# Attention in a two-block hybrid layer stack: products on the whole TensorE array, and the causal mask as a POOL select

## The chip, the cores and the metric

The kernel runs on one core of a Trainium2 chip as one launch. The metric is the time on the device in microseconds, taken as the median of the runs. The core has five engines with queues of their own: TensorE for products, VectorE, ScalarE and GpSimd (POOL) for the rest, and SyncE, which issues the DMAs.

## What is computed

256 tokens of 1024 channels go through a first block (a gated delta rule, a linear recurrent unit and an MLP), get 16 meta tokens put before them, and go through two layers of a second block. Each of these layers is a SwiGLU, a mixer and another SwiGLU. The change touches the mixer, and in it the attention with 8 heads of 64 channels:

```python
proj = u @ w_in
q, k, v, a, b, g_sb, g_conv = jnp.split(proj, IN_SPLITS, axis=-1)
y_sb = stick_breaking_attention(q, k, v) @ w_attn_out
y_conv = conformer_conv(a, b, conv_w, conv_b, conv_ln_g, conv_ln_b) @ w_conv_out
m = jax.nn.sigmoid(g_sb) * y_sb + jax.nn.sigmoid(g_conv) * y_conv
return m @ w_out
# stick_breaking_attention, z = q k^T / sqrt(64), valid = key < query:
log_keep = jnp.where(valid, jax.nn.log_sigmoid(-z), 0.0)
after = lax.cumsum(log_keep, axis=3, reverse=True) - log_keep
attn = jnp.where(valid, jnp.exp(jax.nn.log_sigmoid(z) + after), 0.0)
out = attn @ v
```

So each weight is sigmoid(z) times the product of sigmoid(-z) over the keys between key and query, and keys at or behind the query count as 1 in the product and as 0 in the result.

## The kernel before

**The weight stream.** All weight matrices come from memory in one fixed order, in chunks of 2048 columns, and are cut into units of up to eight 128x128 tiles. ScalarE rounds a unit to its high part (`wh`, float32r), VectorE or, for some units (`POOLED`, line 32), POOL takes the difference (`wl`, line 284 and line 491). TensorE makes three products for each tile, high by high, high by low and low by high (lines 532 to 534, in `job`), over the 272 or 256 tokens. This stream is nearly all of TensorE's work.

**The order of issue.** Every engine works its queue in order, and the order is laid out when the program is built, by a planner in the kernel: each helper (`act`, `tt`, `mm`, `tr` and others) adds an expected cost to its engine's clock by `op` (line 249). Side work is written as generators (`start_flow`, line 332), which `tick` (line 384) advances after each tile of the stream when the operands are expected to be ready. Splits of weights are laid out up to three units ahead of TensorE (`emit_split`, line 481). The conv steps of the mixer are fillers: they are laid wherever VectorE's clock isn't ahead of TensorE's.

**The mixer (from line 1458).** Channels are on the partitions, tokens on the columns. Jobs of the stream come in this order: a and b, q and k, v, the gates gc and gs (8 tiles each), then `ys` (attention output), `yc` (conv output) and `o2`. The side work is the conv over 31 taps on VectorE (`conv`, line 1520), its layer norm, the values, and the heads. Scratch comes from one tile, `arena` (line 146), and nine slots of temporaries, `tmp` (line 378).

- `keep` (line 1494) copies a finished query tile from PSUM to `QT`; a tile of 128 channels holds two heads, one on partitions 0 to 63 and one on 64 to 127.
- `values` (line 1568) transposes the values and scales them into `VN`.
- `head` (line 1582) does one head: for each block of query tokens (16, 128 and 128 in layer 0, 128 and 128 in layer 1) the scores against all keys up to the block's end, over 16, 144 and 272 columns, with 64 rows of the array; then a bfloat16 product of the identity with a mask of -1e30, added to the scores; two sigmoids on ScalarE, a scan and a multiplication on VectorE, transposes on TensorE, three copies on ScalarE, and three products with the values, each with a stationary operand of 64 columns, into the head's half of the partitions of a bank that both heads of a pair share.
- `heads` (line 1658) runs the heads of one parity one after the other; the two parities are two flows.

## Time and profile before

| | us |
|---|---|
| median of 3 timed runs | 1558.58 |
| lowest and highest of them | 1553.17, 1559.71 |
| span of the profiled execution | 1560.1 |
| TensorE busy in it | 1528.2 |
| VectorE busy | 1065.3 |
| ScalarE busy | 800.1 |
| POOL busy | 164.4 |

For the profiled execution the page gives the span, from the first to the last instruction, and no time of its own beside it; the runs of the median are other executions of the same program. TensorE's busy time counts an instruction from its start to its modelled end, and neighbours overlap, so the pace of the products is read from the distance between starts. The granted clock stands as a share of the full 2.4 GHz, of which 1.2 GHz is the other level; its mean over the span is 0.988.

### The profile page before, as it was taken

The numbers are of one execution on the slowest core, as the hardware profiler recorded it, in microseconds if no ns is written. First come the engines' busy times: TensorE is split into PE (matmuls) and PEld (weight loads), VectorE is DVE, ScalarE is ACT, GpSimd is POOL, SyncE is SP. The second block draws the span as 40 slices with busy tenths as digits, with TensorE's granted clock in tenths as the row PEclk, the third lists the DMA queues.
The fourth block names the chain that finished last, engine by engine and source line by source line (L and its number), as shares of the span: only waits on it lengthen the run. The fifth ranks groups of instructions, "written<-read, shape, count | busy, mean of one in ns | idle before, by whom it ended". The sixth has DMA issues, their size and how long they took to land.

```text
span 1560.1 us, 29338 instructions
## 1 busy us (share of the span) xinstructions
PE 1528.2 (98%) x12160; PEld 1488.3 (95%) x12160; DVE 1065.3 (68%) x1884; ACT 800.1 (51%) x1351; POOL 164.4 (11%) x146
## 2 busy tenths in 40 slices
PE   7999999999999999999999999999999999999997
PEld 7898999999999999889999999999999989999997
DVE  5887866667555578877765555655558976866654
ACT  4568666544444444545544444444444555555443
POOL 3230300000000011114400000000001113500000
PEclk8999999999999999999999999999999999999999
DMA  6312555554545543323555454554554423555552
GB/s 227 136 55 82 184 187 183 183 184 164 188 163 176 176 162 135 136 86 131 175 178 188 155 174 157 191 187 160 172 183 160 162 84 109 175 204 190 183 174 76
DMA packets 36373, 248.75 MB, mean 159 GB/s; under 512 B 3984, under 2 KB 5264, under 8 KB 12304
## 3 DMA queue, kind: packets, MB, share of 16 engines
q1 hardware_dynamic: 35248, 245.63, 44.5%
q8 instruction: 95, 1.56, 0.4%
q10 hardware_dynamic: 992, 1.26, 0.2%
q14 instruction: 38, 0.31, 0.1%
HBM read 245.82 MB, written 1.05 MB: 158 GB/s over the span
## 4 chain that ended last, share of the span: by engine, by line
PE 90%; DVE 6%; ACT 2%; issue 1%; POOL 0%; DMA 0%; POOLq 0%; DVEq 0%; SPq 0%; ACTq 0%
PE bank L532 28%; PE bank L534 27%; PE bank L533 27%; PE bank L315 6%; DVE arena L295 2%; DVE arena L284 1%; PE bank L319 1%; DVE wl L284 1%; ACT arena L272 1%; DVE H L284 1%; ACT wh L272 1%; DVE x L284 0%; DMA H<-in_xt_dram 0%; POOL acc L307 0%; DVE co L284 0%
## 5 line engine op out<-in xcount | busy, mean ns | idle before, releaser
L532 PE MATMUL bank<-x,wh 128*128 128x272 f32 (+1 forms) x2624 | 766.9, 292 | 11.5 <-ACT x L272 10.6
L534 PE MATMUL bank<-x,wl 128*128 128x272 f32 (+1 forms) x2624 | 756.0, 288 | 3.6 <-DVE wl L284 3.4
L533 PE MATMUL bank<-x,wh 128*128 128x272 f32 (+1 forms) x2624 | 754.7, 288 | 2.3 <-DVE x L284 1.6
L284 DVE TENSOR_TENSOR wl<-raw,wh 128x1024 fp32r<-128x1024 f32 (+4 forms) x453 | 528.5, 1168 | 207.0 <-PE bank L534 168.8
L272 ACT ACTIVATE wh<-raw 128x1024 fp32r<-128x1024 f32 (+4 forms) x510 | 495.6, 977 | 279.6 <-PE bank L533 219.7
L532 PEld LDWEIGHTS bank<-x,wh 128*128 128x128 f32 x2624 | 500.5, 191 | 16.1 <-ACT x L272 11.7
L533 PEld LDWEIGHTS bank<-x,wh 128*128 128x128 f32 x2624 | 503.4, 192 | 5.0 <-DVE x L284 2.9
L534 PEld LDWEIGHTS bank<-x,wl 128*128 128x128 f32 x2624 | 500.1, 191 | 4.7 <-DVE wl L284 4.7
L534 PE MATMUL bank<-hid,wl 128*128 128x272 f32 (+1 forms) x960 | 273.8, 285 | 0.0
L532 PE MATMUL bank<-hid,wh 128*128 128x272 f32 (+1 forms) x960 | 273.6, 285 | 0.0
L533 PE MATMUL bank<-hid,wh 128*128 128x272 f32 (+1 forms) x960 | 273.0, 284 | 0.0
L532 PEld LDWEIGHTS bank<-hid,wh 128*128 128x128 f32 x960 | 180.9, 188 | 0.0
L533 PEld LDWEIGHTS bank<-hid,wh 128*128 128x128 f32 x960 | 180.9, 188 | 0.0
L534 PEld LDWEIGHTS bank<-hid,wl 128*128 128x128 f32 x960 | 180.5, 188 | 0.0
L491 POOL TENSOR_TENSOR wl<-raw,wh 128x512 fp32r<-128x512 f32 (+3 forms) x57 | 106.6, 1884 | 321.4 <-ACT wh L272 171.4
L284 DVE TENSOR_TENSOR tmp<-bank,R 128x272 f32<-128x272 f32 (+1 forms) x184 | 78.8, 430 | 69.2 <-PE bank L534 66.9
L272 ACT ACTIVATE tmp<-tmp 128x272 f32<-128x272 f32 (+1 forms) x140 | 59.3, 425 | 115.4 <-DVE tmp L284 78.5
L295 DVE SCALAR_TENSOR_TENSOR bank<-arena,C,bank 128x272 f32<-128x272 f32 (+1 forms) x232 | 102.0, 492 | 4.9 <-ACT bank L272 3.8
L1482 POOL MEMSET arena<- 128x1 f32 x10 | 0.5, 99 | 779.1 <-PE bank L534 779.1
L315 PE MATMUL bank<-arena 128*128 128x128 f32 (+7 forms) x528 | 77.6, 286 | 1.1 <-ACT arena L272 0.9
L284 DVE TENSOR_TENSOR hid<-tmp,hid 128x272 fp32r<-128x272 f32 (+1 forms) x120 | 51.7, 433 | 38.1 <-ACT hid L272 38.1
L272 ACT ACTIVATE x<-H,C 128x272 fp32r<-128x272 f32 (+2 forms) x64 | 30.0, 486 | 87.7 <-DVE H L284 87.2
(210 smaller groups left out, 1068.4 us busy)
## 6 DMA issues: line engine op xcount, KB each, us to landing
raw<-in_w_dram SPq DMA_DIRECT2D x187, 1024.0 KB, 4.8
raw<-in_w_dram SPq DMA_DIRECT2D x32, 960.0 KB, 4.7
raw<-in_w_dram SPq DMA_DIRECT2D x16, 896.0 KB, 4.6
raw<-in_w_dram SPq DMA_DIRECT2D x2, 512.0 KB, 5.9
H<-in_xt_dram SPq DMA_DIRECT2D x1, 544.0 KB, 6.6
LG<-in_lgw_dram SPq DMA_DIRECT2D x1, 512.0 KB, 6.3
out_dram<-H SPq DMA_DIRECT2D x2, 256.0 KB, 2.2
LM<-in_cm_dram SPq DMA_DIRECT2D x1, 448.0 KB, 5.5
```

Source lines behind the costliest of these rows:

```text
L272: nc.scalar.activation(out, in_, func, scale=scale, **kw)
L284: nc.vector.tensor_tensor(out=out, in0=a, in1=b, op=fn)
L295: nc.vector.scalar_tensor_tensor(out=out, in0=a, scalar=s, in1=b, op0=op0, op1=op1)
L315: nc.tensor.matmul(out, lhsT, rhs, start=start, stop=stop)
L319: nc.tensor.transpose(out, in_, identity)
L491: nc.gpsimd.tensor_tensor(out=lo[:, 0:n], in0=raw[c][:, o:o + n], in1=wh[i][:, 0:n].bitcast(F32), op=SUB)
L532: nc.tensor.matmul(acc, h[:, s], xh, start=first and done == 0, stop=False)
L533: nc.tensor.matmul(acc, h[:, s], xl, start=False, stop=False)
L534: nc.tensor.matmul(acc, lo[:, s], xh, start=False, stop=last and done == total - 1)
L1482: nc.gpsimd.memset(a.f[:, w:w + 1], 1.0)
```

## The change

The queries are copied into two tiles `QZ`, each with one head of a pair and zeros on the other 64 partitions, so that a score product uses all 128 rows and always 128 columns of the array. The values of a head stand in `VZ` between columns of zeros, so that a product with a 128-column slice writes all 128 partitions of the pair's bank, and the six products of both heads add up in it. The first key block's weights go to `AM`, whose 112 other partitions are zeros. These tiles are filled with zeros by POOL at the start of each mixer. The mask product is gone; instead POOL sets the upper triangle of the two score maps after the sigmoids, to 1 in the one and to 0 in the other. One of the copies goes to a temporary slot instead of the arena. Comments and docstrings that were dropped are left out here.

```diff
-MIX2 = 14560
+MIX2 = 16200
...
-    identb = const.tile([128, 128], BF16, name="identb")
-    maskb = const.tile([128, 128], BF16, name="maskb")
...
-        QT, KT, VT = arena.get(4, T2), arena.get(4, T2), arena.get(4, T2)
+        KT, VT = arena.get(4, T2), arena.get(4, T2)
+        QZ = [arena.get(4, n) for _ in range(2)]
...
-        VN = arena.get(3, 512)
-        if not ready_b[0]:
-            vcopy(identb, ident)
-            vcopy(maskb, M[:, 2])
-            ready_b[0] = True
+        VZ = arena.get(3, 4, 192)
+        AM = [arena.get(n) for _ in range(2)]
+        for i in range(2):
+            nc.gpsimd.memset(QZ[i].f[64 * (1 - i):64 * (1 - i) + 64], 0.0)
+            nc.gpsimd.memset(AM[i].f, 0.0)
+        nc.gpsimd.memset(VZ.f, 0.0)
...
+        def keep_q(t, b, ev):
+            for i in range(2):
+                p = slice(64 * i, 64 * i + 64)
+                cp(QZ[i].f[p, t], b[p, 0:n])
+            give(b)
+            note(ev)
+            yield "V"
...
-                act(VN.f[0:sn, i], b[0:sn], AF.Copy, scale=RC[0:sn, i:i + 1])
+                for par in range(2):
+                    p = slice(64 * par, 64 * par + 64)
+                    act(VZ.f[0:sn, i, :, 128 * par:128 * par + 64], v4(b[0:sn])[:, :, p], AF.Copy, scale=RC[0:sn, i:i + 1])
...
+        def before(a, fill):
+            nc.gpsimd.affine_select(
+                out=a, in_=a, pattern=[[-1, a.shape[-1]]], compare_op=ALU.is_gt, fill=fill, base=0,
+                channel_multiplier=1,
+            )
+            op("G", 0.15 + 0.001 * a.shape[-1])
...
-                z = b[0:tn, col:col + S]
-                mm(z, QT.f[p0:p0 + 64, hp, t0 - o:t0 - o + tn], KT.f[p0:p0 + 64, hp, 0:S], stop=False)
-                mm(z[:, t0:S], identb[0:tn, 0:tn], maskb[0:tn, 0:tn], start=False)
+                mm(b[:, col:col + S], QZ[par].f[:, hp, t0 - o:t0 - o + 128], KT.f[:, hp, 0:S])
...
                 act(a.f[0:tn, 0:S], z, AF.Sigmoid, scale=RP[0:tn, bi:bi + 1])
+                before(keeps[i][0:tn, t0:S], 1.0)
+                before(a.f[0:tn, t0:S], 0.0)
...
-            at_b = arena.get(656)
-            at = at_b.f
+            at_b = arena.get(128)
+            at = yield from slot()
...
-            cp(at[0:NM, 384:384 + n], b1[0:NM, 0:n])
-            cp(at[:, 256:384], b1[:, 288:416])
+            cp(AM[par].f[0:NM], b1[0:NM, 0:n])
+            cp(at_b.f, b1[:, 288:416])
...
-            vs = slice(128 * hp + p0, 128 * hp + p0 + 64)
+            V = VZ.f[:, :, hp, 64 * par:64 * par + 128]
             e = n - 256
-            mm(py[p0:p0 + 64, 0:n], VN.f[0:NM, 0, vs], at[0:NM, 384:384 + n], stop=False)
-            mm(py[p0:p0 + 64, e:n], VN.f[:, 1, vs], at[:, 0:256], start=False, stop=False)
-            mm(py[p0:p0 + 64, e + 128:n], VN.f[:, 2, vs], at[:, 256:384], start=False)
+            mm(py[:, 0:n], V[:, 0], AM[par].f, pairs[hp][1] == 0, False)
+            mm(py[:, e:n], V[:, 1], at[:, 0:256], False, False)
+            mm(py[:, e + 128:n], V[:, 2], at_b.f, False, pairs[hp][1] == 1)
             at_b.done()
+            free_tmps.append(at)
...
-            start_flow(keep(QT.f[:, t, 0:n], job("q", x, n, o), ev_q[t]))
+            start_flow(keep_q(t, job("q", x, n, o), ev_q[t]))
```

## Rows read from the trace of the kernel before

**Rows 1.** This is the first part of the page: busy time of each engine, its share of the span, and the count of its instructions (PE is TensorE, PEld its weight loads, DVE VectorE, ACT ScalarE, POOL GpSimd).

```profile
PE 1528.2 (98%) x12160; PEld 1488.3 (95%) x12160; DVE 1065.3 (68%) x1884; ACT 800.1 (51%) x1351; POOL 164.4 (11%) x146
```

**Rows 2.** This is the fourth part of the page: the shares of the engines in the chain of work that ended last.

```profile
PE 90%; DVE 6%; ACT 2%; issue 1%; POOL 0%; DMA 0%; POOLq 0%; DVEq 0%; SPq 0%; ACTq 0%
```

**Rows 3.** This is the windows view of four stretches: start and end in us, length, then busy time and instruction count of PE, PEld, DVE, ACT and POOL, the granted clock, the DMA share and GB/s. The first and third are the stretches of the heads in layer 0 and layer 1, the second and fourth what follows them up to the end of the gates.

```profile
598.00:692.00 94.00, 94.00 (x654) 79.62 (x653) 76.31 (x166) 49.34 (x119) 11.96 (x5) 0.98 0.32 113
692.00:716.00 24.00, 24.00 (x186) 23.51 (x185) 14.16 (x39) 9.84 (x20) 5.25 (x3) 1.00 0.27 91
1204.00:1294.00 90.00, 90.00 (x639) 77.66 (x638) 76.55 (x158) 48.73 (x104) 11.92 (x5) 0.98 0.35 124
1294.00:1316.00 22.00, 21.88 (x179) 21.47 (x179) 15.09 (x36) 10.59 (x24) 4.98 (x3) 1.00 0.29 104
```

**Rows 4.** This is the timeline of TensorE in layer 0 around the score products of one head: start in us, duration of one or end of the last less start of the first where several are merged, engine, line, operation, operands, tile shape, count. L315 is the helper of the kernel's own products, L532 to L534 the weight stream. A product in float32 (not float32r) is two instructions.

```profile
647.20 0.29 PE L532 MATMUL bank<-x,wh 128*128 128x272 f32 x1
...
647.45 0.29 PE L534 MATMUL bank<-x,wl 128*128 128x272 f32 x1
647.67 0.21 PE L315 MATMUL bank<-arena 64*16 64x16 f32 x2
...
648.51 0.72 PE L315 MATMUL bank<-arena 64*128 64x272 f32 x2
...
649.21 0.37 PE L532 MATMUL bank<-x,wh 128*128 128x272 f32 x1
649.41 0.29 PE L533 MATMUL bank<-x,wh 128*128 128x272 f32 x1
```

**Rows 5.** This is the timeline of TensorE at three places where float32 products use all 128 rows: the layer norm's means, a sum over the channels, and the transposes of a head in layer 1 (two of these five have 16 columns).

```profile
700.33 2.00 PE L315 MATMUL bank<-arena,mean 128*128 128x272 f32 x8
...
702.29 0.28 PE L533 MATMUL bank<-x,wh 128*128 128x272 f32 x1
...
568.12 0.72 PE L315 MATMUL bank<-ones,acc 128*128 128x1 f32 x6
...
568.92 0.29 PE L533 MATMUL bank<-x,wh 128*128 128x272 f32 x1
...
1253.53 0.71 PE L319 MATMUL bank<-M,arena 128*16 128x128 f32 x5
...
1254.20 0.28 PE L533 MATMUL bank<-x,wh 128*128 128x256 f32 x1
```

**Rows 6.** This is the same view in layer 1: the stream products before and behind one head's score products (from 1246.22 to 1247.93) and one head's value products (from 1256.08 to 1257.88).

```profile
1246.22 0.28 PE L534 MATMUL bank<-x,wl 128*128 128x256 f32 x1
...
1247.93 0.28 PE L533 MATMUL bank<-x,wh 128*128 128x256 f32 x1
...
1255.84 0.28 PE L532 MATMUL bank<-x,wh 128*128 128x256 f32 x1
...
1256.08 0.28 PE L534 MATMUL bank<-x,wl 128*128 128x256 f32 x1
...
1257.88 0.28 PE L533 MATMUL bank<-x,wh 128*128 128x256 f32 x1
```

**Rows 7.** This is the same view in layer 0: the stream products before and behind the value products of one head (666.08 and 667.92) and of two heads in a row (638.98 and 642.22).

```profile
666.08 0.29 PE L534 MATMUL bank<-x,wl 128*128 128x272 f32 x1
...
667.92 0.29 PE L533 MATMUL bank<-x,wh 128*128 128x272 f32 x1
...
638.98 0.29 PE L534 MATMUL bank<-x,wl 128*128 128x272 f32 x1
...
642.22 0.29 PE L533 MATMUL bank<-x,wh 128*128 128x272 f32 x1
```

**Rows 8.** This is the same view at the first two heads of layer 0, those of the first pair: the first product of each, and the first stream product behind them.

```profile
598.96 0.21 PE L315 MATMUL bank<-arena 64*16 64x16 f32 x2
...
600.62 0.21 PE L315 MATMUL bank<-arena 64*16 64x16 f32 x2
...
602.15 0.52 PE L532 MATMUL bank<-x,wh 128*128 128x272 f32 x1
```

**Rows 9.** This is the windows view in slices of 2 us, columns as above; the granted clock is the number behind the busy times.

```profile
602.00:604.00 2.00, 2.00 (x10) 1.89 (x10) 1.78 (x6) 2.00 (x9) 0.00 (x0) 0.56 0.76 320
604.00:606.00 2.00, 2.00 (x12) 2.00 (x11) 1.79 (x5) 2.00 (x4) 0.00 (x0) 0.59 0.00 0
1271.00:1273.00 2.00, 2.00 (x11) 1.91 (x11) 1.76 (x5) 2.00 (x6) 0.00 (x0) 0.56 1.00 393
```

**Rows 10.** This is the view of one source line, the only select on POOL: duration in ns (least, median, greatest), first and last start, shape.

```profile
L926 POOL TENSOR_SCALAR_AFFINE_SELECT arena<-arena x2: 637/728/819, 45.2 to 45.8; 128x512 f32<-128x512 f32 x2
```

**Rows 11.** This is the timeline of POOL at the start of the first mixer.

```profile
562.45 0.27 POOL L1482 MEMSET arena<- 128x1 f32 x6 [380.61 <-PE bank L534]
562.65 0.21 POOL L1483 MEMSET arena<- 128x128 f32 x1
562.82 2.39 POOL L491 TENSOR_TENSOR wl<-raw,wh 128x1024 fp32r<-128x1024 f32 x1
```

**Rows 12.** This is the timeline of VectorE at the same place; in brackets the idle time before and what ended it.

```profile
562.43 0.44 DVE L284 TENSOR_TENSOR tmp<-bank,R 128x272 f32<-128x272 f32 x1 [1.07 <-PE bank L534]
562.91 2.60 DVE L284 TENSOR_TENSOR H<-H,tmp 128x272 f32<-128x272 f32 x1
```

**Rows 13.** This is the chain that ended last, in order of time, at the same place: start, length, engine and what it writes.

```profile
562.91 2.60 DVE H L284
```

More of the change, by code (lines that the diff above doesn't have):

```diff
@@ L1454, in swiglu @@
         return nx, ev_sq, phase
-    ready_b = [False]
     def mixer(x, ev_r, layer, next_g, old_phase):
@@ L1580, in mixer @@
         pairs = {}
+        def before(a, fill):
[4 more added lines that the diff above has]
+            op("G", 0.15 + 0.001 * a.shape[-1])
         def head(hp, par):
-            p0 = 64 * par
             yield from wait(ev_q[hp], ev_k[hp])
```

## The prediction, made before the changed kernel was run

> **What bounds the kernel now.** I read the busy times first: TensorE is busy for 1528.2 of 1560.1 us, VectorE for 1065.3, ScalarE for 800.1 [rows 1]. The chain that ended last is 90% TensorE and 6% VectorE [rows 2]. So TensorE's queue sets the time, and the change has to be priced by what it does to that queue. Busy time doesn't give this price, since a TensorE counted busy may be changing over between products; the distances between starts do, so I read the timeline next.
>
> The eight heads of a layer lie between the products of the weight stream in 598 to 692 and 1204 to 1294 us. TensorE is busy in all of both; VectorE, next, for 76.3 of 94.0 and 76.6 of 90.0 us [rows 3]. That is the second thing to see: VectorE has 17.7 and 13.4 us of air there, and a TensorE that becomes 11 us faster uses up most of it.
>
> **The products.** One head of layer 0 alone: the stream product before it starts at 647.45, the second one after it at 649.41 [rows 4]. In these 1.96 us lie the head's nine instructions and two stream products. Stream products by themselves start 0.125 us apart (647.20 to 647.45 are two), so the head takes 1.96 - 2x0.125 = 1.71 us. The reader should see where it goes: the last pair of 64-row products over 272 columns with its mask product takes 649.21 - 648.51 = 0.70 us, and the first stream product behind them 0.20 instead of 0.125.
>
> With full operands the same arithmetic stands elsewhere in the trace. Eight 128x128 products over 272 columns and one stream product run from 700.33 to 702.29: (1.96 - 0.125)/8 = 0.229 us each. Six over one column take (0.80 - 0.125)/6 = 0.112 each, five over 128 columns (0.67 - 0.12)/5 = 0.110 each, the changeover behind them counted in [rows 5]. I scale 144 columns to 0.121 and 256 to 0.215. A float32 product is two instructions, so a head's scores cost 2x(0.112 + 0.121 + 0.229) = 0.92 us; the 16-column block's stationary operand grows from 16 to 128 columns and is counted at 0.112. The saving is 1.71 - 0.92 = 0.79 us a head, 6.3 us in layer 0. Layer 1 has two blocks: 1247.93 - 1246.22 - 2x0.12 = 1.47 us [rows 6] against 0.70, 0.77 a head, 6.2 us.
>
> The value products of one head alone in layer 0: 667.92 - 666.08 - 0.25 = 1.59 us; of two heads in a row: 642.22 - 638.98 - 0.25 = 2.99 [rows 7]. Padded they take 2x(0.229 + 0.215 + 0.110) = 1.11. The saving is 0.48 alone and 0.385 in a row; eight heads give 3.1 to 3.8 by how they lie, I take 3.3. In layer 1: 1257.88 - 1256.08 - 0.24 = 1.56 [rows 6] against 2x(0.215 + 0.215 + 0.110) = 1.08, 0.48 alone, 3.4 with a like mix. Transposes keep their form.
>
> Sum on TensorE: 6.3 + 3.3 + 6.2 + 3.4 = **19.2 us**, all in a queue that never idles there.
>
> A rule speaks against padding: the Trainium skill, TensorEngine Tiling (Array Packing), section Theoretical Speedup, says that products with a small side can run as independent tiles, up to twice as fast. By it the two heads of a pair would share the array, a pair of score products would take one head's time instead of the padded 1.85, a pair of value products 1.39 instead of 2.22, and padding would lose some 9 us. The row decides: the second head of a pair starts at 600.62, when the first, begun at 598.96, is through, and the next stream product at 602.15 [rows 8]. They ran in turn, 1.6 us each, so there is no overlap to lose.
>
> **The clock.** Behind these two heads the granted clock falls to 0.56 in 602 to 604 and 0.59 in 604 to 606, that is 1.2 GHz for most of it; the same begins at 1271 [rows 9]. It costs 2x0.44 + 2x0.41 = 1.7 us of full-speed work each time, 3.4 together. TensorE was busy without a pause before [rows 3]; what it did was partial-array products one after the other. I take it that full-array products keep 2.4 GHz and **3.4 us** come back; the lower bound is nothing.
>
> On this the Trainium skill, TensorE: Matmul & The Clock Gate, Part 1, says that the rate follows how busy the engine has been. By that rule a TensorE busy throughout would not have fallen, the cause would lie elsewhere, and the sum would lack the 3.4. The row shows a fall without a pause, so busy time alone doesn't explain it.
>
> **POOL and VectorE.** Each block's two score maps get a select on POOL: 48 in layer 0 (16 of them 16x16), 32 in layer 1. The nearest row is a 128x512 select, 0.73 us [rows 10]. With a fixed part of about 0.10 (six one-column fills overlap in 0.27 us [rows 11]) 128 columns come to 0.26; bounds are 0.21, the 128-column fill [rows 11], and 0.73, if width doesn't count. I take 0.26: 32x0.26 + 16x0.12 = 10.2 us of POOL in layer 0, 8.3 in layer 1, where it now works 12 us of 94 and of 90 [rows 3]. A select stands between ScalarE's sigmoid and VectorE's scan, and on POOL it is in order with weight splits of 2.39 us [rows 11]: it waits for a split ahead of it, and a split behind it waits for the sigmoid. Splits are laid out up to three units ahead of TensorE's (some 9 us), which covers a late split; conv steps cover a late scan. Without that cover it is 2.4 us a hit.
>
> POOL also stops VectorE: H<-H,tmp, with both operands in SBUF, takes 2.60 us, where the step before it over as many columns took 0.44; it starts at 562.91, inside POOL's split of 562.82, and ends with it [rows 11, 12]. Selects will do this too, shorter. About half of VectorE's time is such operations; I charge a third of the select time, 3 us a layer (from 0 to all of it). VectorE then has 79.3 and 79.6 us against a TensorE of 94.0 - 9.6 - 1.7 = 82.7 and 90.0 - 9.6 - 1.7 = 78.7. In layer 0 it fits, in layer 1 it misses by 1. Its conv work may slip into 692 to 716 and 1294 to 1316, where it works 14.2 and 15.1 us [rows 3], but two queues of fixed order that are nearly full wait for each other. I charge TensorE waits of 1 us in layer 0 and 3 in layer 1, **4 us** given back; the bounds are 0 and the whole saving.
>
> **The start of each mixer.** Fills of QZ, AM and VZ (1088, 1088, 272, 272 and 2304 columns) come to stand on POOL ahead of the split at 562.82. By the 128-column fill of 0.21 us they take 4.8 us with the fixed part, up to 8.2 without. No row shows fills beside such VectorE steps; they read nothing, so I take it that they don't stop it. Then H<-H,tmp, which is on the chain that ended last [rows 13], loses its 2.16 us of waiting. But the split, now later, will stop two-operand steps of the norm behind it, on which TensorE waits as well: I keep 0.6 a layer, **1.2 us** (up to 4.3 if the split meets nothing, -4 if fills do stop VectorE).
>
> **At nothing:** two ScalarE copies for each query tile and each block of values instead of one, 7 more a layer at the stretch's mean of 0.41 us, hidden by a ScalarE that works 49 of 94 us [rows 3] (2.9 us without that cover); two VectorE casts dropped; a temporary slot in place of a wide arena block; AM reused by the next head of its parity, whose copy waits for products long issued. DMA issues and SP's queue don't change.
>
> **Sum:** -19.2 - 3.4 - 1.2 + 4 = -19.8 us on 1560.1. The three timed runs have a median of 1558.6 and reach from 1553.2 to 1559.7; the profiled execution, of which only the span is given, lies 1.5 above the median. Off the median it is 1538.8; I round to **1540 us**.
>
> **Rivals.**
> VectorE becomes the bound: it keeps half of its air, 8.9 and 6.7 us, so the stretches end at 88 and 86 us instead of 94 and 90. Gain 5.8 + 3.7 + 1.2, 1548. For it: 81% and 85% busy now. Against it: it has other stages to slip into. Chance 0.18.
>
> The clock still falls: 3.4 less, 1543; inside the forecast, a quarter of it.
>
> Given back: the next stage stops TensorE by as much, since the conv norm arrives no earlier than now, 1555 to 1559. Against it: some 20 us of other products lie between the last head and the first product that reads the heads' results [rows 3]. Chance 0.10. That padding doesn't give the full form can hardly be, since the operands are whole.
>
> Slower: a 128-column select costs what the 512-column one does, 0.73 us. Then POOL has 35 and 23 us of selects, and VectorE, stopped for half to all of that, needs 94 to 111 and 88 to 100 us in stretches of 94 and 90: midway 13 us more than now, less 3.4 and 1.2, 1567. It decides from about 0.45 us a select. Against it: fills grow with width [rows 11]. Chance 0.07. The tiling rule's 1568 has 0.02.
>
> **Numbers.** The forecast (gain of 12 to 26) has 0.63. Faster by over 0.5%, 7.8 us and about what a measurement of this kernel can tell from no change: 0.63 and two thirds of 0.18, 0.75. Within 0.5%: 0.16. Slower: 0.09. The range goes from 1532, with all bounds in my favour, past the VectorE case to 1552; it leaves out the last rivals and a part of the tail below.
>
> **What would show it.** Scores of a head at 0.92 us with no mask product, and a stream product 0.125 behind; value products at 1.11; a granted clock of 1.00 at the heads; selects near 0.26; H<-H,tmp at 0.44. Wrong if selects take over 0.45, or if TensorE idles for VectorE's scans or splits by more than 10 us.

## The result, and the profile after

The changed kernel takes 1544.0 us (median of 6 runs, 1538.9 to 1550.1) beside 1555.9 us for the kernel before in the same set: a ratio of 0.9916, 95% interval 0.9888 to 0.9943. Two later sets of 6 runs gave 0.9894 (0.9866 to 0.9922) and 0.9915 (0.9895 to 0.9936). So it is about 0.9% faster, some 14 us; 1540 had been forecast with a range of 1532 to 1552. The profiled execution took 1550.1 us, the slowest of its six; its span is 1548.4 us, against 1560.1 us before.

The first part of the page after, to be read beside [rows 1]:

```profile
PE 1507.0 (97%) x12120; PEld 1486.7 (96%) x12120; DVE 1076.3 (70%) x1882; ACT 804.1 (52%) x1365; POOL 197.6 (13%) x236
```

TensorE is busy for 21.2 us less, but the span is only 11.7 us shorter: 9.5 us came back as pauses. Some 4 us of the 21.2 are not the change's: they belong to a pace of the last gate and up products that differs between executions of one program (last section). Where the pauses lie is seen in the windows view of the changed kernel, with the columns of [rows 3]:

```profile
598.00:692.00 94.00, 93.24 (x710) 89.70 (x710) 84.57 (x169) 53.82 (x126) 29.80 (x54) 1.00 0.38 134
692.00:716.00 24.00, 23.99 (x181) 22.95 (x181) 19.58 (x48) 8.77 (x21) 6.58 (x6) 1.00 0.26 89
1204.00:1294.00 90.00, 87.82 (x690) 84.83 (x688) 83.97 (x161) 52.05 (x114) 25.37 (x34) 1.00 0.39 136
1294.00:1316.00 22.00, 21.32 (x178) 21.12 (x178) 14.49 (x38) 13.38 (x25) 11.54 (x9) 1.00 0.32 109
```

In the heads' stretches TensorE issues more instructions in the same time (710 and 690 instead of 654 and 639), the granted clock stays at 1.00, and VectorE has gone from 76.3 and 76.6 to 84.6 and 84.0 us. TensorE, which never paused there before, now does.

**A single head.** TensorE's timeline after, around the scores of a head in layer 0, the values of one, and the scores of one in layer 1, answering to [rows 4, 6, 7]:

```profile
649.92 0.29 PE L532 MATMUL bank<-x,wl 128*128 128x272 f32 x1
650.04 1.09 PE L315 MATMUL bank<-arena 128*128 128x16 f32 x6
650.77 0.49 PE L530 MATMUL bank<-x,wh 128*128 128x272 f32 x1
651.10 0.29 PE L531 MATMUL bank<-x,wh 128*128 128x272 f32 x1
...
672.88 0.29 PE L532 MATMUL bank<-x,wl 128*128 128x272 f32 x1
...
674.25 0.29 PE L531 MATMUL bank<-x,wh 128*128 128x272 f32 x1
...
1244.23 0.28 PE L532 MATMUL bank<-x,wl 128*128 128x256 f32 x1
1244.35 0.86 PE L315 MATMUL bank<-arena 128*128 128x144 f32 x4
1244.85 0.48 PE L530 MATMUL bank<-x,wh 128*128 128x256 f32 x1
1245.17 0.28 PE L531 MATMUL bank<-x,wh 128*128 128x256 f32 x1
```

Read as the prediction read them, from the stream product before to the second one behind, less two of the stream's distances: scores 651.10 - 649.92 - 0.25 = 0.93 us (0.92 forecast), values 674.25 - 672.88 - 0.25 = 1.12 (1.11 forecast), scores in layer 1 1245.17 - 1244.23 - 0.24 = 0.70 (0.70 forecast). One sub-claim failed: the first stream product behind the scores starts its successor 0.33 us later (650.77 to 651.10), not 0.125. The changeover is dearer than before, when it was 0.20 us [rows 4]. The sum came out all the same, since the forecast had worked out its price of 0.92 us from rows with the changeover counted in [rows 5].

**Stretch by stretch.** The stream's 11,136 products come in the same order in every kernel, so their starts serve as a ruler. Four stretches hold all of the change: the 528 products up to the 32nd of each mixer ("ahead"), and the 1,248 from there on ("mixer"; a mixer has 1,248). The boundary lies about 4 us into the mixer, so that TensorE's wait for the last part of the mixer's input, which comes before the mixer's 22nd product, falls into "ahead"; the 528 products up to the mixer's first take 66.3 us in every kernel. This table is worked out from the starts of those products in each profile; pauses are TensorE's, over 0.2 us.

| profile | ahead 1 | mixer 1 | ahead 2 | mixer 2 | sum | pauses in mixer 1 / 2 |
|---|---|---|---|---|---|---|
| before | 68.0 | 201.7 | 68.0 | 191.2 | 528.9 | 1.6 / 1.9 |
| changed, first profile | 66.3 | 197.2 | 66.3 | 188.4 | 518.2 | 4.4 / 9.1 |
| changed, `again` | 66.3 | 195.7 | 66.3 | 188.5 | 516.7 | 4.4 / 9.2 |
| changed, `again_2` | 66.3 | 195.7 | 66.3 | 188.3 | 516.6 | 4.4 / 9.2 |
| `no_select` | 66.3 | 194.6 | 66.3 | 186.4 | 513.6 | 3.2 / 8.4 |
| `mask_product` | 66.3 | 195.9 | 66.3 | 189.5 | 518.0 | 5.1 / 8.0 |
| `half_select` | 68.0 | 199.7 | 68.0 | 186.6 | 522.3 | 3.0 / 3.1 |
| `o2_on_vector` | 66.3 | 195.7 | 66.3 | 183.4 | 511.6 | 4.4 / 7.0 |
| `b_on_vector` | 66.3 | 193.8 | 66.3 | 185.9 | 512.3 | 2.6 / 8.0 |
| `both_on_vector` | 66.3 | 193.2 | 66.3 | 182.1 | 508.0 | 3.2 / 4.3 |
| `both_2` | 66.3 | 193.8 | 66.3 | 182.9 | 509.4 | 2.6 / 4.2 |
| `late_fills` | 68.0 | 194.2 | 68.0 | 187.8 | 518.0 | 2.9 / 8.0 |
| `both_half_taps` | 66.3 | 189.4 | 66.3 | 181.3 | 503.4 | 1.4 / 3.5 |
| `none_in_heads` | 66.3 | 197.4 | 66.3 | 187.8 | 517.9 | 5.8 / 7.7 |

The rest of the span differs between executions of one kernel by several us, for reasons shown at the end; that is why the sums of these stretches tell more than single spans.

**Where the pauses are.** Three kinds of them make most of the difference, and behind each stands the same thing: a weight split on POOL that reads two tiles, and a VectorE step that meets it and ends with it, or up to 0.3 us behind it.

At the start of the mixer (POOL's timeline, then VectorE's, then the waits of TensorE in 562 to 598), answering to [rows 11, 12]:

```profile
565.18 1.00 POOL L1471 MEMSET arena<- 64x1088 f32 x1 [381.95 <-PE bank L532]
566.24 0.33 POOL L1472 MEMSET arena<- 128x272 f32 x1
566.51 1.00 POOL L1471 MEMSET arena<- 64x1088 f32 x1
567.46 0.32 POOL L1472 MEMSET arena<- 128x272 f32 x1
567.73 2.02 POOL L1473 MEMSET arena<- 128x2304 f32 x1
...
570.07 2.38 POOL L489 TENSOR_TENSOR wl<-raw,wh 128x1024 fp32r<-128x1024 f32 x1
```

```profile
565.59 0.44 DVE L284 TENSOR_TENSOR H<-H,tmp 128x272 f32<-128x272 f32 x1
...
570.02 2.46 DVE L291 TENSOR_SCALAR rs_y<-RC 128x3 int32<-128x3 int32 x1
```

```profile
PE bank L315 <- DVE RC L295: 1.4, 1, 1.4
```

H<-H,tmp, stopped for 2.60 us before, takes 0.44 us in the middle of a fill, in the second mixer as well: the fills don't stop it. But the split behind them is now late enough to meet a step over three columns, which takes 2.46 us, and TensorE waits for the norm's RC. In the kernel before the step took 0.17 us (VectorE's timeline):

```profile
569.08 0.17 DVE L291 TENSOR_SCALAR rs_y<-RC 128x3 int32<-128x3 int32 x1
```

At o2 of the second layer (VectorE, POOL, TensorE's waits in 1294 to 1360):

```profile
1330.77 2.57 DVE L284 TENSOR_TENSOR x<-arena,x 128x256 fp32r<-128x256 f32 x1
```

```profile
1330.66 2.39 POOL L489 TENSOR_TENSOR wl<-raw,wh 128x1024 fp32r<-128x1024 f32 x1 [2.76 <-ACT wh L272]
```

```profile
PE bank L531 <- DVE x L284: 4.5, 3, 3.7
```

The same step of the kernel before was ahead of the same split by a hair and took 0.42 us (its VectorE and POOL timelines):

```profile
1342.95 0.42 DVE L284 TENSOR_TENSOR x<-arena,x 128x256 fp32r<-128x256 f32 x1
```

```profile
1343.23 5.76 POOL L491 TENSOR_TENSOR wl<-raw,wh 128x1024 fp32r<-128x1024 f32 x2 [3.14 <-PE bank L534]
```

Ahead by 0.28 us it costs nothing, behind by 0.11 us it costs TensorE a pause of 3.7 us, and the granted clock behind the pause is 0.66 for 10 us (1330:1340 below) where the kernel before had 0.98 and 0.85 in its two slices (shown there too).

Inside the heads' stretches it is the scans (VectorE and POOL of the changed kernel):

```profile
1250.07 1.93 DVE L311 TENSOR_TENSOR_SCAN arena<-tmp,onesrow 128x144 f32<-128x144 f32 x1
```

```profile
1249.07 2.61 POOL L489 TENSOR_TENSOR wl<-raw,wh 128x1024 fp32r<-128x1024 f32 x1 [0.73 <-ACT wh L272]
```

Such a scan takes 0.45 us by itself; TensorE's transposes then wait for the head's tiles, 0.7 us in the first mixer and 2.2 us in the second, nothing before (TensorE's waits in 598 to 692, then in 1204 to 1294):

```profile
PE bank L319 <- DVE arena L284: 0.7, 1, 0.7
...
PE bank L319 <- DVE arena L284: 2.2, 4, 0.8
```

Of the 2.2 us, 0.6 (at 1246.8) have no stopped step ahead of them; there the head's scan stands behind other work of VectorE.

The Trainium skill, SBUF — State Buffer, section Who interferes with whom, says that a VectorE instruction with two SBUF inputs contends with a GpSimd instruction that reads SBUF, not with one that only writes it, that VectorE's fast forms of one-input operations can contend too, and that whoever starts first keeps the other out to its end. The rows agree on the first point: 0.44 us beside a fill, 1.93 and 2.57 us beside a split. The three-column step has one input and took 2.46 us; whether it ran in a fast form is not shown here. On the order the rows are not sharp: in the first mixer that step's record starts 0.05 us ahead of the split's (570.02 and 570.07), in the second 0.17 us behind it, and both times it was held to the split's end.

**The clock.** The windows view of the changed kernel in slices of 10 us, at the heads and at o2; the granted clock is the number behind the busy times:

```profile
600.00:610.00 10.00, 10.00 (x79) 9.84 (x78) 5.88 (x15) 5.96 (x17) 2.90 (x12) 1.00 0.39 143
1270.00:1280.00 10.00, 9.46 (x79) 9.14 (x78) 9.65 (x22) 6.55 (x15) 4.50 (x8) 1.00 0.30 107
...
1330.00:1340.00 10.00, 6.61 (x33) 6.61 (x34) 7.58 (x7) 5.01 (x8) 5.71 (x3) 0.66 0.56 201
```

The kernel before at o2:

```profile
1330.00:1340.00 10.00, 8.73 (x67) 8.13 (x66) 9.83 (x19) 4.32 (x10) 4.19 (x4) 0.98 0.31 109
1340.00:1350.00 10.00, 10.00 (x74) 9.87 (x73) 7.67 (x10) 6.88 (x10) 6.21 (x4) 0.85 0.61 212
```

The two falls at the heads [rows 9] are gone. Behind o2's pause the grant is 0.66 in the mean of the slice, so two thirds of it ran at 1.2 GHz and not at 2.4; in the kernel before it was half as long.

### The profile page after: what moved, and what is told of

The parts are those of the page before. It is cut to its first block, busy times and chain, and to the rows that moved or that the text cites. A ratio compares the mean times of both kernels' runs of the same rounds, so it can differ in the third digit from the quotient of the medians.

```text
span 1548.4 us, 29451 instructions
## 1 busy us (share of the span) xinstructions
PE 1507.0 (97%) x12120; PEld 1486.7 (96%) x12120; DVE 1076.3 (70%) x1882; ACT 804.1 (52%) x1365; POOL 197.6 (13%) x236
## 5 line engine op out<-in xcount | busy, mean ns | idle before, releaser
L532 PE MATMUL bank<-x,wl 128*128 128x272 f32 (+1 forms) x2624 | 754.0, 287 | 3.4 <-DVE wl L284 3.3
L530 PEld LDWEIGHTS bank<-x,wh 128*128 128x128 f32 x2624 | 500.7, 191 | 12.3 <-ACT x L272 9.3
L532 PEld LDWEIGHTS bank<-x,wl 128*128 128x128 f32 x2624 | 501.1, 191 | 4.5 <-DVE wl L284 4.5
L532 PE MATMUL bank<-hid,wl 128*128 128x272 f32 (+1 forms) x960 | 273.8, 285 | 0.0
L532 PEld LDWEIGHTS bank<-hid,wl 128*128 128x128 f32 x960 | 180.5, 188 | 0.0
L1471 POOL MEMSET arena<- 64x1088 f32 (+1 forms) x4 | 3.9, 975 | 780.5 <-PE bank L532 780.5
L272 ACT ACTIVATE hid<-tmp 128x272 fp32r<-128x272 f32 (+1 forms) x120 | 51.0, 426 | 42.3 <-DVE tmp L284 40.6
```

What stands on the lines that cost most here:

```text
L272: nc.scalar.activation(out, in_, func, scale=scale, **kw)
L530: nc.tensor.matmul(acc, h[:, s], xh, start=first and done == 0, stop=False)
L532: nc.tensor.matmul(acc, lo[:, s], xh, start=False, stop=last and done == total - 1)
L1471: nc.gpsimd.memset(QZ[i].f[64 * (1 - i):64 * (1 - i) + 64], 0.0)
```

## The experiments

**The changed kernel twice more, on two chips.** No edit.

> The changed kernel once more, unaltered, for a second profile and a closer ratio. First theory: the products shortened by the padding are worth about 16 us of TensorE time (its products other than the stream's took 34.6 + 30.5 us in the two mixers before and 26.5 + 22.2 us after), and VectorE, filled up by the same work in less time, gives back about 10 us in waits of TensorE for single late steps (TensorE idle in the two mixers 3.7 us before, 13.8 us after). It expects 0.992 of the time before (0.990 to 0.994), 1543 to 1546 us. Two things are open in the first profile of the changed kernel: its last gate and up products came every 113.3 ns where those before came every 117.8 ns (4.7 us over the stage), and the last low part of o2's input in the second layer was stopped for 2.57 us behind a split on POOL (TensorE idle 3.7 us). If the pace belongs to the program, it is 113 ns here again; if to the execution, 117.8 ns is as likely. If the stop hangs on which of two starts comes first by 0.1 us, it may be gone here, and the span then some 5 us shorter.

Measured: 1539.9 us, 0.9894 (0.9866 to 0.9922), a little better than expected. Pauses and stretches came out as in the first profile (see the table), the 3.7 us stop too: it belongs to the program, though the two starts are 0.1 us apart. The paces of the 256-column stages did not: see the last section.

> The changed kernel beside the version with three splits moved, on the same chip. Expected 0.991 of the time before (0.988 to 0.993), as in its first two sets of runs. The stretches of the stream in its profile: 195.7 to 197.2 us in the first mixer, 188.4 us in the second, as in both earlier profiles. The stages of 256 columns (the MLP's products ahead of 270 us, the last gate and up products) come at 113 or at 118 ns a product, by chance: each pace appeared in each of the two stages in two profiles of the same kernel.

Measured: 1544.6 us, 0.9915 (0.9895 to 0.9936), as expected.

**No selects.** The order of all other work is the same, instruction by instruction.

```
         def before(a, fill):
-            nc.gpsimd.affine_select(
-                out=a, in_=a, pattern=[[-1, a.shape[-1]]], compare_op=ALU.is_gt, fill=fill, base=0,
-                channel_multiplier=1,
-            )
             op("G", 0.15 + 0.001 * a.shape[-1])
```

> The changed kernel without its POOL selects (attention is then not causal); the order in which all other work is laid out stays as in the changed kernel. First theory (VectorE is full, the selects cost nothing of their own): within 2 us of the changed kernel, 1542 to 1546 us. Rival (the selects, as one more step between ScalarE's sigmoids and VectorE's scans, make the heads late, and that is what gives the gain back): at least 5 us faster than the changed kernel, 1539 us or less, with the waits of TensorE's transposes for the heads' arena tiles (0.7 us in the first mixer, 2.2 us in the second) gone.

Measured: 1540.3 us, 0.9889 (0.9858 to 0.9920), where the changed kernel had 1539.9 on the same chip. The four stretches are 3.1 us shorter than in `again`: the transposes wait 1.8 us in all instead of 2.9, and behind o2's pause, which stays, the clock is low for 3.4 us instead of 6.8, which is 1.7 us of work. So the selects cost at most about 3 us, and the timed runs can't tell it from nothing; the rival's 5 us are not there. The 1.5 us that the second layer's transposes still wait stand behind a multiplication of two tiles that meets a split (2.33 us instead of 0.44), so it need not be the scan. The by-form view of POOL in 598 to 692 of the changed kernel prices them:

```profile
L1593 POOL TENSOR_SCALAR_AFFINE_SELECT arena<-arena 128x128 f32<-128x128 f32 x16 | 6.8, 426 | 0.5
L1593 POOL TENSOR_SCALAR_AFFINE_SELECT tmp<-tmp 128x128 f32<-128x128 f32 x16 | 5.7, 358 | 0.8
```

By the view of the line, the median of one is 0.29 us; the means of 0.36 and 0.43 hold the few that met something, up to 1.38 us.

**Each half of the change alone.** First the padding with the mask's product (and a scratch 128 columns smaller, to make room for the two constants):

```
-                mm(b[:, col:col + S], QZ[par].f[:, hp, t0 - o:t0 - o + 128], KT.f[:, hp, 0:S])
+                mm(b[:, col:col + S], QZ[par].f[:, hp, t0 - o:t0 - o + 128], KT.f[:, hp, 0:S], stop=False)
+                mm(b[:, col + t0:col + S], identb, maskb[:, 0:tn], start=False)
...
-                before(keeps[i][0:tn, t0:S], 1.0)
-                before(a.f[0:tn, t0:S], 0.0)
```

> The changed kernel with the mask as a bfloat16 product again (over the whole array) in place of the selects; the padded scores and values stay. First theory: the mask products took 2.6 us of TensorE in the first mixer and 1.9 us in the second before, so this is 4 to 5 us slower than the changed kernel, 1548 us, and still 7 us faster than before; the gain of the padding stays without POOL's part. Rival (the selects give the gain back): faster than the changed kernel by up to 5 us in spite of the products, 1539 to 1543 us. The constants of the mask stand where they stood before, and so do all fixed inputs of the stream: if their place sets the pace of the last gate and up products, it is 117.8 ns here, and not 113.3 ns.

Measured: 1548.8 us, 0.9945 (0.9925 to 0.9965). Then the selects with the 64-row products of before:

```
-                mm(z, QT.f[p0:p0 + 64, hp, t0 - o:t0 - o + tn], KT.f[p0:p0 + 64, hp, 0:S], stop=False)
-                mm(z[:, t0:S], identb[0:tn, 0:tn], maskb[0:tn, 0:tn], start=False)
+                mm(z, QT.f[p0:p0 + 64, hp, t0 - o:t0 - o + tn], KT.f[p0:p0 + 64, hp, 0:S])
...
+                before(keeps[i][0:tn, t0:S], 1.0)
+                before(a.f[0:tn, t0:S], 0.0)
```

> The kernel before with the selects in place of the mask's products, and nothing else of the change: scores and values stay on 64 rows and 64 columns, no zeros are written. First theory: it is worth the 4.5 us that the mask products took, 1551 us, and the granted clock still falls at the heads of both layers (0.56 and 0.59 before), since the partial products stay. Rival (the selects make the heads late): no faster than before, 1556 us or more.

Measured: 1554.2 us, 0.9972 (0.9952 to 0.9992). Padding alone is worth 0.55%, the selects alone 0.28%, the two together 0.85 to 1.06%: within their intervals, which are as wide as the differences, they add up. In the stretches of the profiles they don't: 10.9 us and 6.6 us alone, 10.7 to 12.3 together. With other operations to place, the planner also lays out the side work anew, and pauses and falls of the clock differ. On TensorE's queue the attention's runs (each from the stream product before to the second behind, less two distances and the pauses, summed over both mixers) take 62.6 us before, 54.9 with the selects alone, 48.5 with the padding alone, 44.9 with both. The mask products of a head between partial float32 products thus cost 7.7/16 = 0.48 us, twice what they cost between full ones (3.6/16 = 0.23).

Half of the expectation for `half_select` failed, and it tells something: the windows view of that kernel has no fall at the heads, though its products are partial.

```profile
600.00:610.00 10.00, 10.00 (x76) 9.07 (x75) 8.29 (x14) 7.08 (x18) 5.29 (x13) 1.00 0.30 107
1270.00:1280.00 10.00, 10.00 (x80) 9.08 (x79) 9.58 (x17) 5.93 (x14) 5.06 (x5) 1.00 0.41 154
```

`mask_product` has none there either. So in these profiles either half of the change takes the falls away. That they need partial products and mask products together is suggested by this and not shown: there is one profile each of `half_select` and of the kernel before, and falls come and go between executions of one program (the changed kernel's first profile has one in 570 to 580 that `again` and `again_2` lack). With span times one less the granted clock as its price, the lower clock cost 14.1 us in the mean of the 12 timed runs of `half_select` and 16.3 us in the 20 of the kernel before on the same chip, single runs scattering by some 3 us: the same way, but little beyond the scatter. The pace of the last gate and up products was 118 ns in both, which by itself would have fitted the idea that the constants' place sets it; `again`, with the places of the changed kernel, had 118 ns too, so it does not.

**The meetings.** Three splits go from POOL to VectorE: 435, of the second layer's o2, and 179 and 381, the first b tile of each mixer that went to POOL. Here all three; `o2_on_vector` has the first alone, `b_on_vector` the other two:

```
         on_pool.update(mine[every - 1::every])
+    on_pool -= {179, 381, 435}
```

> The changed kernel with one weight split moved from POOL to VectorE: the second layer's o2 tile whose split started on POOL 0.1 us ahead of the last low part of o2's input and stopped it for 2.57 us (TensorE then idle for 3.7 us, in both profiles of the changed kernel and in those without the selects and with the mask product; not in the kernel before nor with the partial products, where the low part came first). First theory (that one meeting gives back what the heads of the second layer gained): the 3.7 us and most of the slower clock behind them go, the second mixer's stretch of the stream falls from 188.4 us to 183 to 184 us, and the whole is 4 to 5.5 us faster than the changed kernel. Rival (VectorE is full, so the split only moves the lateness to VectorE): 1 us faster at most, the wait for the low part replaced by waits for weights or for x.

Measured: the second mixer falls from 188.4 to 183.4 us, as expected. A wait of 1.6 us for x stays at o2; ahead of that input VectorE's own queue has a split of 1.23 us. The whole, 0.9905 (0.9887 to 0.9923), can't be told from the changed kernel's ratios on other chips, so the 4 to 5.5 us expected of it were not shown there.

> The changed kernel with one weight split of each mixer moved from POOL to VectorE: the first b tile that goes to POOL, which in the changed kernel stands behind the fills and stops the norm's small steps for 2.46 us (TensorE idle 1.45 and 1.23 us for RC). First theory (the fills cost nothing themselves; they only moved the split from one victim to the next): those waits go, and the slower clock behind the first; 3 to 4 us faster than the changed kernel if nothing else is late. The split now stands ahead of the mixer's last input on VectorE, for 1.2 us: if that is what TensorE waits for instead, 1 us faster at most. Rival (the fills themselves hold VectorE up): no gain, RC still late.

Measured: 0.9886 (0.9862 to 0.9910); the pauses for RC are gone in both mixers, and the four stretches are 4.3 us shorter than in `again_2`; 1.7 us of that is a shorter fall of the clock at o2, whose pause of 3.7 us stayed. The split ahead of the mixer's last input costs nothing that can be seen (66.3 us in the stretches ahead, as without it).

> Both moves together (three splits from POOL to VectorE). First theory: the two add up, 7 to 9 us faster than the changed kernel, about 1534 us, 0.984 of the time before. Rival (VectorE is the bound): no faster than the better of the two alone.

Measured: 0.9877 (0.9856 to 0.9899), 1543.3 us on a chip where the kernel before took 1562.7. The four stretches add up to 508.0 us, 8.6 less than in `again_2`. The ratio is short of the 0.984 expected, which lies below its interval.

> The version with three splits moved from POOL to VectorE, on the same chip as the changed kernel. First theory (the give-back is two meetings of VectorE steps with POOL splits, per layer one at the mixer's start and one at o2 of the second layer): its profile showed 193.2 us and 182.1 us for the two mixers, 3.3 us and 6.3 us less than the changed kernel, so 6 to 9 us faster than that, 0.985 to 0.987 of the time before. Rival (VectorE is the bound and the profile was a lucky one): within 2 us of the changed kernel.

Measured, beside the changed kernel on one chip: 1537.8 us against 1544.6 us; 0.9868 (0.9846 to 0.9889) against 0.9915 (0.9895 to 0.9936). This is the fastest of all, 0.5% ahead of the changed kernel. VectorE at o2 there:

```profile
1325.48 0.42 DVE L284 TENSOR_TENSOR x<-arena,x 128x256 fp32r<-128x256 f32 x1
1325.81 2.35 DVE L284 TENSOR_TENSOR wl<-raw,wh 128x1024 fp32r<-128x1024 f32 x2
```

The low part takes 0.42 us again, with the moved split behind it. With the three splits moved, the waits for RC are gone in both mixers, and at o2 the pause of 3.7 us and one of the two stretches of lower clock: that these meetings were a price of the change is shown by this.

**The fills later.** The three lines of zeros go behind the first a and b products.

```
-        for i in range(2):
-            nc.gpsimd.memset(QZ[i].f[64 * (1 - i):64 * (1 - i) + 64], 0.0)
-            nc.gpsimd.memset(AM[i].f, 0.0)
-        nc.gpsimd.memset(VZ.f, 0.0)
...
                 start_flow(layer_norm(), 1)
+                for i in range(2):
+                    nc.gpsimd.memset(QZ[i].f[64 * (1 - i):64 * (1 - i) + 64], 0.0)
+                    nc.gpsimd.memset(AM[i].f, 0.0)
+                nc.gpsimd.memset(VZ.f, 0.0)
```

> The changed kernel with the fills of the mixer (zeros for q, the first block's probabilities and the values) issued after the first a and b products instead of ahead of them, so that the first split on POOL starts where it did before. First theory: the start of the mixers looks as in the kernel before (H<-H,tmp stopped for 2.6 us, TensorE idle 1.07 and 1.02 us there, the last stretch ahead of each mixer 68.0 us instead of 66.3 us), the waits for RC (1.45 and 1.23 us) and the slower clock behind the first go: between 2 us faster and 1 us slower than the changed kernel. The stop of o2's input in the second layer (3.7 us) stays, since it does not depend on the fills. Rival (the fills cost VectorE or TensorE time themselves): the waits come again where the fills now stand.

Measured: 1549.3 us, 0.9927 (0.9907 to 0.9946). The stretches ahead are 68.0 us again, the pauses for RC are gone, o2's 3.71 us stay: as expected. The sum of the stretches, 518.0 us, is 1.4 us above `again_2`'s, a little more than expected. So the zeros cost POOL 4.7 us and TensorE nothing that can be seen; they decide which step the split behind them meets.

**VectorE with air.** From `both_2`, the convolution's taps 16 to 30 left out:

```
-                for k in range(1, 31):
-                    dst = Y.f[:, t, 0:n] if k == 30 else y
+                for k in range(1, 16):
+                    dst = Y.f[:, t, 0:n] if k == 15 else y
```

> The version with three splits moved, with 15 of the convolution's 30 later taps left out in each mixer, so that VectorE has about 30 us less to do in each heads' stretch. It asks how much of the time VectorE's fullness still costs. First theory: little; the waits of the transposes for the heads' arena tiles go (0.4 us in the first mixer, 2.2 us in the second) and with them the wait for co (0.7 us), so the two mixers take 192 and 179 to 180 us instead of 193.2 and 182.1 us. Rival (VectorE is what sets the pace of the heads' stretches): over 5 us less in each mixer.

Measured (one profile): 189.4 and 181.3 us, 4.4 and 1.6 less than `both_2`: in the first mixer nearer to the rival's 5 us, in the second nearer to the first theory. In the first mixer 1.2 us are pauses and 1.7 us a fall of the clock in 734 to 738 that `both_2` has and this profile has not; the remaining 1.5 us aren't assigned. `both_on_vector`, the same program as `both_2`, has no such fall either. The transposes of the second layer still wait 1.5 us, with scans of 2.14 and 2.58 us inside POOL splits, while VectorE sat idle ahead of them. Those waits are not from a full VectorE.

**No POOL splits at the heads.** From `both_2`, the rest of the mixers' first tiles on VectorE as well:

```
-POOLED = [(("a", "b", "q", "k", "v", "gc", "gs"), 4), (("ys", "o2"), 2), (("yc", ), 1), (("o1b",), 2), (("K", "Q"), 8)]
+POOLED = [(("ys", "o2"), 2), (("yc", ), 1), (("o1b",), 2), (("K", "Q"), 8)]
```

> The version with three splits moved, with the remaining POOL splits of the mixers' a, b, q, k, v and gate tiles on VectorE as well (about five more in each layer, some 6 us of VectorE's work at 1.22 us each), so that no two-input operation of POOL meets a head's scan. In both_half_taps the transposes of the second layer still waited 1.5 us, each time behind a scan stopped by a POOL split (2.14 and 2.58 us instead of 0.45 us), though VectorE had half its convolution to do. First theory (it is such meetings that give time back, not VectorE's fullness): no scan takes over 1 us, the transposes' waits (0.4 and 2.2 us) go, and the two mixers take 193 and 180 to 181 us, up to 3 us less in all than with the three splits moved; VectorE busy above 9.6 of 10 us in the heads' stretches. Rival (VectorE is full): the added 6 us do not fit, convolution and layer norm come late, TensorE waits for the conv path, and each mixer takes 2 to 6 us longer.

Measured: 1547.1 us, 0.9926 (0.9907 to 0.9946). Both theories were right about their own part. The lines view of VectorE in the second heads' stretch has the scans of the changed kernel at 0.75 us in the mean, and here at 0.46:

```profile
L311 DVE TENSOR_TENSOR_SCAN arena<-tmp,onesrow 128x144 f32<-128x144 f32 x8 | 6.0, 749 | 0.0
```

```profile
L311 DVE TENSOR_TENSOR_SCAN arena<-tmp,onesrow 128x144 f32<-128x144 f32 x8 | 3.7, 461 | 0.0
```

and no transpose waits. But the layer norm and the conv path come late (TensorE's waits in 560 to 770, then in 1160 to 1370):

```profile
PE bank L531 <- ACT co L272: 2.9, 1, 2.9
PE bank L315 <- DVE nr L295: 2.3, 1, 2.3
...
PE bank L531 <- ACT co L272: 2.8, 1, 2.8
PE bank L315 <- DVE nr L295: 2.6, 1, 2.6
```

The moved splits were eight in a layer, not the five expected, 9.8 us of VectorE's work at 1.22 us each, and they don't fit, as the wait for co of 0.7 us in the changed kernel had hinted. Behind each of these pairs of waits the clock is low for 10.2 us, where `both_2` has 3.4 us in each mixer. The POOL splits at the heads are worth their price.

## Why the prediction was right, step by step

The range held, and so did the mechanism of the largest gain, but every term came out worse than forecast, by 7.0 us in all. That the median is 4 us from 1540, and not 7, owes something to the base: the kernel before had 1555.9 us in the set of six, and 1558.6 in the three runs that the forecast started from.

| term | forecast | measured, changed kernel (`again`) |
|---|---|---|
| products | -19.2 | -17.7 |
| falls of the clock at the heads | -3.4 | -3.4, and +1.7 behind o2's pause |
| start of the mixers, net | -1.2 | -0.7 |
| given back in pauses | +4 | +7.3 |
| sum | -19.8 | -12.8 (the stretches: -12.2) |

**Products.** The price of a head was right to 0.01 us: 0.92, 0.70 and 1.11 us forecast, 0.93, 0.70 and 1.12 measured, from the full-array rows of other work [rows 5]. Summed over all runs it is 62.6 - 44.9 = 17.7 us and not 19.2. Where the 1.5 us went isn't assigned: the runs are 44, beside 43 before, so it is not that the heads lie by themselves more often. The padding alone (`mask_product`) shortened the attention's runs by 62.6 - 48.5 = 14.1 us. The rule of the Trainium skill, TensorEngine Tiling (Array Packing), section Theoretical Speedup, by which partial tiles run side by side and padding would lose some 9 us, is not borne out here: the first pair of heads ran in turn [rows 8], and the values of two heads in a row took 2.99 us where those of one took 1.59 [rows 7]. The 1.39 us for a pair of value products and the 9 us stand in the prediction without their working.

**Clock.** The falls at the heads went as forecast, and no profile with padded products has one there. The reason given, "full-array products keep 2.4 GHz", may be too narrow: the one profile of `half_select` has partial products and no fall at the heads. And the 3.4 us were counted as free, but a pause can bring a slower clock elsewhere: behind o2's pause 0.66 was granted over 10 us, 3.4 us of full-speed work (0.4 of them while TensorE still stood), where the kernel before lost 1.7 us. All of this is read from single profiles. Over the executions whose clock is on record, the lower clock cost the kernel before 16.2 us in the mean of 53 (9.3 to 21.9) and the changed kernel 15.1 us in the mean of 18 (9.2 to 20.1), priced as for `half_select`: 1.1 us less, which fits -3.4 + 1.7 = -1.7 within the scatter. In the first profile another fall (0.83 in 570 to 580) followed RC's pause; in `again` and `again_2` it did not.

**Start.** H<-H,tmp lost its stop (0.44 us), and this was worth more than charged: 1.7 us in each stretch ahead, 3.4 in all, since TensorE's pause of 1.1 us there went with it. The split did meet the norm's steps behind it, though the one that it stopped has one operand and not two as written, and took back 1.45 and 1.23 us. Net 0.7 us. The fills, 4.7 us on POOL, were estimated at 4.8 and "don't stop" VectorE, which the row now shows for H<-H,tmp.

**Given back.** This step failed in size. The 4 us were argued from two full queues of fixed order that wait for each other, spread over both layers. Measured: pauses in the mixers grew by 1.3 us in the first and 6.0 in the second, RC's left out. Of these 7.3 us, 3.7 are one meeting at o2 of the second layer, behind the heads, and 2.9 are transposes that wait, all but 0.6 of it behind scans that met splits; co adds 0.5. VectorE's share of busy time alone didn't decide these: `both_half_taps` left 1.5 of the transposes' 2.6 us, and `both_2` removed o2's pause with VectorE's work increased. With the meetings at RC and o2 taken away, the four stretches are 19.5 to 20.9 us shorter than before, and the whole 0.9868, some 20 us: what the change had to give without them.

**Rivals.** VectorE as the bound (1548) did not come in, but it is near: `none_in_heads`. The slow select (1567) is out, at 0.29 us by the median against 0.26 estimated and 0.45 as its point of decision. With the selects VectorE is busy 0.8 and 2.1 us longer in the two mixers than without (`again` beside `no_select`), where 3 us a layer were charged. "Given back in the next stage" is the rival that came in by a half, by another mechanism than the late norm it named.

## What to carry to other kernels

A head's price could be taken to a hundredth of a microsecond from other products of the same form in the trace, with the distance between starts read and the changeover behind it counted; the sum over all heads was still 1.5 of 19.2 us off. What a saving gives back is not read from busy shares: list the steps on the way to the bound engine that another engine's long operation can stop, and see by how little each escapes now, since shifting all of them by a few microseconds deals those meetings anew. After such a change look at the new pauses one by one; moving three of the 52 POOL splits of the two mixers was worth half as much again as the change.

## What was not expected of the hardware

The stream's 256-column products have two paces in the stages that read x, and an execution takes one or the other for a whole stage. The windows view of two stages, in the first profile of the changed kernel and then in `again`, the same program:

```profile
190.00:270.00 80.00, 80.00 (x682) 80.00 (x681) 53.99 (x85) 51.01 (x88) 0.00 (x0) 1.00 0.53 188
1380.00:1470.00 90.00, 90.00 (x797) 90.00 (x796) 58.59 (x83) 47.11 (x67) 0.00 (x0) 1.00 0.55 195
```

```profile
190.00:270.00 80.00, 80.00 (x706) 80.00 (x706) 58.37 (x95) 55.39 (x96) 0.00 (x0) 1.00 0.57 203
1380.00:1470.00 90.00, 90.00 (x767) 90.00 (x766) 56.25 (x81) 45.17 (x64) 0.00 (x0) 1.00 0.51 183
```

80 us over 682 or 706 products is 117.3 or 113.3 ns, 90 over 767 or 797 is 117.3 or 112.9, all with TensorE busy throughout and a granted clock of 1.00. One program showed both paces in both stages, in opposite order. The last gate and up stage has 1,056 products, so a pace is worth some 4.3 us there; the 768 products of the earlier stage some 3.1 us. This is a part of the spread of single runs. Another is the granted clock: in the six runs of the first set, from 1550.1 down to 1538.9 us, the lower clock cost 20.1 us in the slowest and 12.3 in the fastest, so it goes with most of those 11 us; over all sets the two go together less closely. The pace made the first profile of the changed kernel look 4 us better in its last stage than the change had made it. What selects the pace stays open: the program's layout does not, since one program shows both. The 272-column stages show one pace only (125 to 126 ns in all profiles).
